# Gate products moved into the last recurrence, index transposes moved later, and gathers beside the dense group paced by the TensorE time of each piece

## The chip, the cores and the metric

The kernel runs on one core of one Trainium2 chip. The metric is device time in microseconds, of one execution of the whole program. The core has five engines with a queue of their own each: TensorE (PE, with PEld for its weight loads), VectorE (DVE), ScalarE (ACT), GpSimd (POOL) and SyncE (SP, which here only issues transfers). An instruction waits at the head of its queue, and what is behind it on that engine waits too.

## The reference

One layer on 1024 tokens of 1024 channels: a gated MLP over chunks of 128 tokens (gMLP), a state-space branch (SSD) over the same chunks, a gated merge with layer norm, and a PEER layer: each token picks, per head, the 16 best of 128 x 128 experts by two sets of keys, and uses those rows of two tables of 16384 x 1024.

```python
h = x @ w_in[i]
uv, z, xbc, dt_raw, gate_pre = jnp.split(h, [o1, o2, o3, o4], axis=-1)
gates = jax.nn.sigmoid((gate_pre + b_gate[i])).reshape(bsz, s, N_BRANCHES, d)
ya = gmlp_branch(uv, ...) @ gm_w_out[i]
yb = ssd_branch(z, xbc, dt_raw, ...) @ ssd_w_out[i]
merged = gates[..., 0, :] * ya + gates[..., 1, :] * yb
x1 = layer_norm(DEEPNORM_ALPHA * x + merged @ w_o[i], ln1_g[i], ln1_b[i])
ch = peer(x1, peer_w_q[i], peer_k1[i], peer_k2[i], peer_u[i], peer_v[i])
ple_gate = jax.nn.sigmoid(x1 @ ple_w_gate[i] + ple_b_gate[i])
ple = ple_gate * (p[i] @ ple_w_proj[i])
x = layer_norm(DEEPNORM_ALPHA * x1 + ch + ple, ln2_g[i], ln2_b[i])
```

In the SSD branch a state passes from chunk to chunk, `h = dec * h + st`, and each of 16 pairs of heads needs the state ahead of its chunk. In `peer`, for each token, `act = gelu(u_tab[e] . x) * gate` over its 128 experts, and the output is the sum of `act * v_tab[e]`.

## The kernel before

The 1024 tokens go in three groups: two blocks of 128 tokens, three blocks, three blocks (`GROUPS`). The first two groups are "gather" groups: their PEER rows are fetched one per token by indirect transfers from POOL's queue (L803), 128 x 1024 f32 (0.524 MB) at a time, 128 of `peer_u` and 128 of `peer_v` for each of five blocks, 1280 in all. They land in a ring of 12 slots (`RING`). VectorE multiplies a `peer_u` row with the token (L822); a `peer_v` row goes through TensorE (`product`, L864), four rows at a time. The last group is "dense": it multiplies with all of both tables.

Every large product is done in three fp32r matmuls (`mm3`, L150): a weight tile is loaded by SP, split into `whi` on ScalarE (L146) and `wlo` on VectorE (L147). `channel_major` gives 128 channels by all tokens of a group in a bank of the PSUM pool `mm` (four banks), 24 matmuls; `token_major` gives tokens by 256 channels. Small transposes and products use the pool `mt` (two banks). Tile pools and the order on each engine come from a scheduler that goes by the order of the code as a priority; `tc.high_priority(offset=n)` moves an instruction n places ahead.

`front(gi)` is the program of a group, a generator: the gMLP branch (four products `w_v`; then the `dt` chain of the SSD branch, L261 to L310; eight products `w_u`, each with a small product `pm` into `mix`; eight of `w_g` with `gm_w_out`), the SSD branch (`make_bc`, `make_x`, `core_g`, `core`, for 16 head pairs j), the merge (L509 to L525: gate product `w_g[8 + j]`, sigmoid, times `rrow`, product `ssd_w_out[j, 1]`), `w_o` and layer norm, `ple_w_proj`, transposes of `x1` (L581), 16 products `w_q` with the 16 best keys of each (L590 to L600), and `ple`. `core(j)` has two halves: the first transposes `xs`, makes the states, runs the recurrence into `pv` (L447, with the state of the group before loaded into `pv[:, 0]`, L440) and multiplies `dec` (L453); the second (L461, L464) makes `y`. `rrow` gathers the squares of `y`; `ss` (L503) sums it over partitions after the last pair.

While a group's `front` runs, two other streams are woven in. `beside` steps `select` of the group before (its choice of experts, VectorE work ending in transposes of the index, L739 to L786), three steps at a time. And the main loop at the end of `block_kernel` adds each yielded cost times `SIDE[phase]` to `owed` and steps the gathers (`experts`) while `owed` is above zero; a gather costs 1.47. `UNIT` = 5.35 is the cost of a product over 512 tokens, so 4.01 for three blocks. What is left of `experts` after the last group runs behind it.

`experts` first takes 64 rows of `peer_u` (`PP`), and then merges each half block of `peer_v` with the next 64 of `peer_u`. `transposed` of `actd` (L786, L829) turns a half block's activations for TensorE.

`dense` (group 2, phase 4) goes over 16 blocks of 8 pieces. `piece(i2)` makes `ewh`, `ewl` of 128 experts: for 48 pieces (`AHEAD`, six blocks) the scores were stored in `s_d` earlier and are only loaded; for the others `channel_major(peer_uT)` computes them. In a step, the products `po` of a block with `peer_vd` (18 matmuls of 512 columns each, eight per step) take turns with the pieces of the next block. The six loaded blocks are spread among the ten computed ones: the steps that make the pieces of blocks 5, 4, 3, 2, 1 and 0 are steps 0, 2, 5, 8, 10 and 13. Weight, `s` and `gte` loads are issued by SP.

```python
while side and owed > 0:
    step = next(side[0], None)
    if step is None:
        side.pop(0)
    else:
        owed -= step
```

Of the kernel before, what the change touches and what calls it, by code (L numbers as in the profile page):

```python
# [8 lines left out]
F32 = mybir.dt.float32  # L9
# [46 lines left out]
def take(g, n):  # L56
    for _ in range(n):
        yield next(g)
# [20 lines left out]
def block_kernel(ctx, tc, a, out):  # L79
# [135 lines left out]
    def front(gi):  # L215
# [24 lines left out]
        with tc.tile_pool(name="ga", bufs=1, side=side_) as ga, \  # L240
# [9 lines left out]
            for u in range(4):  # L250
                for cc, p in token_major(a["w_v"][u], xh, xl):
                    A.activation(v[:, cc, u * 256:u * 256 + 256], p, AF.Gelu_apprx_tanh)
                for c in range(NB):
                    V.bn_stats(st[:, c, u, :], v[:, c, u * 256:u * 256 + 256])
                beside()
                yield 2 * unit

            with tc.tile_pool(name="sd", bufs=1, side=side_) as sd:
# [13 lines left out]
                sh = [128, NB, NCOL]  # L272
                dt = xp.tile(sh, F32, name="dt")
                V.tensor_add(dt, pd, dtb[:, None, :].to_broadcast(sh))
                e = sd.tile(sh, F32, name="e")
                A.activation(e, dt, AF.Abs)
                A.activation(e, e, AF.Exp, scale=-1.0)
                r = sd.tile(sh, F32, name="r")
# [4 lines left out]
                q = sd.tile(sh, F32, name="q")  # L283
# [5 lines left out]
                V.tensor_mul(e, dt, nega[:, None, :].to_broadcast(sh))  # L289
                pc = pst.tile([128, 2, NB * NCOL], F32, name="mt", tag="mt")  # L290
# [3 lines left out]
                acs = xp.tile(sh, F32, name="acs")  # L294
                acsf = acs.rearrange("p c h -> p (c h)")
                A.copy(acsf, pc[:, 0, :])
                cdec = xp.tile(sh, F32, name="cdec")
                A.activation(cdec.rearrange("p c h -> p (c h)"), pc[:, 1, :], AF.Exp)
                dtd = xp.tile(sh, F32, name="dtd")
# [6 lines left out]
                act = sd.tile([NB * NCOL, 128], F32, name="q")  # L306
                A.copy(act, pt)
                arow = dram.tile([NCOL, NB, 128], F32, name=f"arow{gi}")
# [13 lines left out]
            gl = ga.tile([128, 8, T], F32R, name="gl")  # L322
            for g in range(8):
# [40 lines left out]
        with tc.tile_pool(name="sa", bufs=1, side=side_) as sa, tc.tile_pool(name="sb", bufs=2, side=side_) as sb:  # L364
# [18 lines left out]
            bT, cT, xs, zs, arows, btok, cbm = [{} for _ in range(7)]  # L383
# [31 lines left out]
            def core(j):  # L415
# [23 lines left out]
                if gi > 0:  # L439
                    DMA.dma_start(pv[:, 0], state_d[gi - 1, j])  # L440

                for c in range(NB if gi < NG - 1 else NB - 1):
# [3 lines left out]
                    for h in range(2):  # L446
                        V.scalar_tensor_tensor(pv[:, (c + 1) % NB, h], pv[:, c, h],  # L447
# [10 lines left out]
                for c in range(NB):  # L458
                    for h in range(2):
# [3 lines left out]
                        if c + gi > 0:  # L463
                            PE.matmul(o, lhsT=pv[:, c, h, :], rhs=ce[:, h, c * 128:c * 128 + 128],  # L464
                                      start=False, stop=True, tile_position=(0, h * 64))
# [23 lines left out]

            yield from make_bc(0)  # L490
            yield from make_x(0)
            for j in range(16):
                if j % 2 == 1 and j < 15:
                    yield from make_bc(j // 2 + 1)
                if j < 15:
                    yield from make_x(j + 1)
# [15 lines left out]
        with tc.tile_pool(name="mb", bufs=2, side=side_) as mb:  # L512
            for j in range(8):
# [4 lines left out]
                pg = channel_major(a["w_g"][8 + j], xh, xl)  # L518
# [42 lines left out]
        with tc.tile_pool(name="qa", bufs=1, side=side_) as qa, tc.tile_pool(name="qb", bufs=2, side=side_) as qb:  # L561

            for c in range(NB):
# [5 lines left out]
                if mode == "gather":  # L569
# [550 lines left out]
```

## Time and profile before

| | us |
|---|---|
| median of 3 runs (lowest, highest) | 3779.35 (3778.96, 3787.96) |
| the profiled execution | 3774.55 |
| its span, first to last instruction | 3772.9 |
| TensorE busy | 3437.7 (91%) |
| VectorE busy | 2936.8 (78%) |
| ScalarE busy | 1756.0 (47%) |
| POOL busy | 1606.3 (43%) |
| mean granted clock of TensorE | 0.955 of full speed |

The busy time of an engine is the time in which it executed something, not a measure of how well. The clock is granted at one of two levels (1.2 and 2.4 GHz); 0.955 means that it was at the lower for 9% of the time. Group 0 ends near 500 us, group 1 near 1350 us; the dense group's products run from 2657.7 to 3757.3 us. The gathers run from 567 to 3662 us. 1184 MB are moved, 314 GB/s on average.

### The profile page before, as it was taken

The page shows a single profiled execution, that of the slowest core. Times are in us where ns is not written, and L with a number is a line of the kernel's source. Part 1 is how long each engine was busy: PE and PEld are TensorE (multiplying, and loading weights), DVE is VectorE, ACT ScalarE, POOL GpSimd, SP SyncE. Part 2 cuts the span into 40 slices and gives each one's busy share as a digit, 9 for nine tenths or more (in the row PEclk, how much of TensorE's full clock was granted, in tenths as well). Part 3 has the DMA queues.
Part 4 walks back from the last instruction along what each step waited for, and adds up shares of the span by engine and source line. Part 5 has one row for each costly group of instructions (what it writes and reads, how often), then busy time and mean ns, then how long its engine had stood idle before and what let it go on. Part 6 is the DMA issues. An engine that isn't in the chain of part 4 may idle for free.

```text
span 3772.9 us, 59493 instructions
## 1 busy us (share of the span) xinstructions
PE 3437.7 (91%) x21390; PEld 2946.2 (78%) x21390; DVE 2936.8 (78%) x6823; ACT 1756.0 (47%) x2675; POOL 1606.3 (43%) x1310
## 2 busy tenths in 40 slices
PE   8898997999989988999988989998889989989988
PEld 8897996988877876888878888777667868667756
DVE  6677799898977989896688999997667766766535
ACT  6788543476843333466652334774222323322223
POOL 0000004756545354554354445443556565665540
PEclk9998998999999988999989999999999999999999
DMA  5453656989879886989888899999999999999992
GB/s 200 161 172 130 238 180 241 389 309 356 317 279 385 309 324 234 356 311 343 305 326 327 298 338 349 362 377 372 360 381 400 395 386 389 368 383 401 356 350 95
DMA packets 409159, 1183.88 MB, mean 314 GB/s; under 512 B 41120, under 2 KB 139424, under 8 KB 405792
## 3 DMA queue, kind: packets, MB, share of 16 engines
q0 software_dynamic: 187488, 682.71, 47.7%
q1 hardware_dynamic: 221376, 497.38, 36.9%
q8 instruction: 168, 2.75, 0.3%
q14 instruction: 127, 1.04, 0.1%
HBM read 1121.01 MB, written 58.92 MB: 313 GB/s over the span
## 4 chain that ended last, share of the span: by engine, by line
PE 33%; DVE 16%; DMA 13%; issue 4%; ACT 1%; POOL 1%; SPq 0%; DVEq 0%; ACTq 0%; POOLq 0%
PE mm L152 6%; PE mm L154 6%; PE mm L153 6%; PE pacc L864 4%; DVE row L822 3%; DVE wlo L147 3%; DMA ew<-s 3%; PE po L152 3%; DMA row<-in_peer_v_dram,idxT 3%; PE po L153 3%; PE po L154 3%; DMA raw<-in_peer_uT_dram 2%; PE mt L947 2%; DMA row<-in_peer_u_dram,idx 1%; DMA raw<-in_peer_vd_dram 1%
## 5 line engine op out<-in xcount | busy, mean ns | idle before, releaser
L146 ACT CAST whi<-raw 128x1024 fp32r<-128x1024 f32 (+1 forms) x676 | 701.1, 1041 | 1192.4 <-PE mm L153 612.0
L803 POOL DMA_INDIRECT row<-in_peer_u_dram,idx x640 | 811.5, 1268 | 874.9 <-PE pacc L864 254.3
L147 DVE TENSOR_TENSOR wlo<-raw,whi 128x1024 fp32r<-128x1024 f32 (+1 forms) x676 | 816.2, 1210 | 375.5 <-ACT whi L146 374.7
L154 PE MATMUL mm<-xh,wlo 128*128 128x384 f32 (+2 forms) x3160 | 1056.4, 335 | 46.7 <-DVE wlo L147 46.7
L152 PE MATMUL mm<-xh,whi 128*128 128x384 f32 (+2 forms) x3160 | 1066.3, 338 | 34.3 <-ACT whi L146 25.6
L803 POOL DMA_INDIRECT row<-in_peer_v_dram,idxT x640 | 780.9, 1220 | 712.0 <-PE pacc L864 232.5
L153 PE MATMUL mm<-xl,whi 128*128 128x384 f32 (+2 forms) x3160 | 1051.9, 333 | 0.6 <-DVE xl L136 0.6
L822 DVE SCALAR_TENSOR_TENSOR row<-row,x1b 128x1024 f32<-128x1024 f32 x640 | 774.6, 1217 | 64.8 <-DMA row<-in_peer_u_dram,idx 58.5
L152 PEld LDWEIGHTS mm<-xh,whi 128*128 128x128 f32 (+1 forms) x3160 | 611.2, 194 | 89.7 <-ACT whi L146 46.1
L154 PEld LDWEIGHTS mm<-xh,wlo 128*128 128x128 f32 (+1 forms) x3160 | 609.8, 193 | 66.4 <-DVE wlo L147 55.0
L153 PEld LDWEIGHTS mm<-xl,whi 128*128 128x128 f32 (+1 forms) x3160 | 610.5, 193 | 12.2 <-issue 6.1
L864 PE MATMUL pacc<-row,zw 128*32 128x512 f32 x2560 | 316.9, 614 | 37.0 <-DMA row<-in_peer_v_dram,idxT 36.8
L152 PE MATMUL po<-whi,ewh 128*128 128x512 f32 x768 | 316.0, 411 | 32.2 <-DVE eacc L1013 32.2
L153 PE MATMUL po<-wlo,ewh 128*128 128x512 f32 x768 | 311.0, 405 | 14.4 <-DVE wlo L147 14.3
L154 PE MATMUL po<-whi,ewl 128*128 128x512 f32 x768 | 309.9, 404 | 0.0
L152 PEld LDWEIGHTS po<-whi,ewh 128*128 128x128 f32 x768 | 148.3, 193 | 104.6 <-DVE eacc L1013 36.1
L864 PEld LDWEIGHTS pacc<-row,zw 128*32 128x32 f32 x2560 | 67.9, 111 | 180.6 <-issue 131.1
L135 ACT CAST ewh<-ew 128x384 fp32r<-128x384 f32 x128 | 65.6, 514 | 296.7 <-DVE ew L985 230.1
L818 POOL DMA_DIRECT2D x1b<-x x5 | 3.0, 601 | 446.4 <-DMA x<-x 446.4
L153 PEld LDWEIGHTS po<-wlo,ewh 128*128 128x128 f32 x768 | 148.5, 193 | 51.0 <-DVE wlo L147 16.8
L154 PEld LDWEIGHTS po<-whi,ewl 128*128 128x128 f32 x768 | 148.1, 193 | 40.9 <-issue 5.0
L153 PE MATMUL mm<-wlo,xh 128*128 128x256 f32 x512 | 147.8, 289 | 11.4 <-DVE wlo L147 11.4
(272 smaller groups left out, 5603.8 us busy)
## 6 DMA issues: line engine op xcount, KB each, us to landing
raw<-in_peer_uT_dram SPq DMA_DIRECT2D x128, 512.0 KB, 8.0
raw<-in_peer_vd_dram SPq DMA_DIRECT2D x128, 512.0 KB, 6.8
raw<-in_w_xbc_dram SPq DMA_DIRECT2D x96, 512.0 KB, 5.9
raw<-in_w_g_dram SPq DMA_DIRECT2D x48, 512.0 KB, 6.7
raw<-in_w_z_dram SPq DMA_DIRECT2D x48, 512.0 KB, 5.4
raw<-in_ssd_w_out_dram SPq DMA_DIRECT2D x48, 512.0 KB, 5.3
raw<-in_w_q_dram SPq DMA_DIRECT2D x48, 512.0 KB, 4.7
g<-gt SPq DMA_DIRECT2D x24, 1024.0 KB, 7.5
```

Of the source, the lines that this page charges most:

```text
L135: A.copy(hi, src)
L146: A.copy(hi, raw)
L147: V.tensor_sub(lo, raw, hi.bitcast(F32))
L152: PE.matmul(p, lhsT=lh, rhs=rh, start=start, stop=False, skip_group_check=skip)
L153: PE.matmul(p, lhsT=lh, rhs=rl, start=False, stop=False, skip_group_check=skip)
L154: PE.matmul(p, lhsT=ll, rhs=rh, start=False, stop=stop, skip_group_check=skip)
L803: g = POOL.indirect_dma_start(out=t, out_offset=None, in_=a[tab], in_offset=bass.IndirectOffsetOnAxis(ap=ix, axis=0))
L818: POOL.dma_start(x1, x1_d[gi, c])
L822: u = V.scalar_tensor_tensor(t, t, 1.0, x1, op0=OP.mult, op1=OP.mult, accum_out=act[:, k:k + 1])
L864: return PE.matmul(pacc[q * 32:q * 32 + 32, h * 512:h * 512 + 512], lhsT=zws[z][:, q, r % 4, :], rhs=ts[q][:, h * 512:h * 512 + 512], star ...
L947: PE.matmul(p[:, i, :], lhsT=o1, rhs=o2, start=True, stop=True)
```

## The change

1. *The `dt` chain* becomes a generator `steps()`, and is stepped once behind each of the products `w_v[1]` to `w_v[3]`, and a last time behind `w_u[0]`.
2. *`w_u`*: the product of `g + 1` stands ahead of the small products of `g` (`make_u`).
3. *The state* of the group before is loaded in `make_x` into a tile of its own, `p0`, and no longer into `pv[:, 0]` in `core`.
4. *The merge's* first three gate products stand between the halves of `core(15)` and around it (`pgs`). Each yields one unit, and the merge's iterations yield two units as before.
5. *`x1`'s stores* are issued by ScalarE's queue, behind `ple_w_proj`; SP issued them inside the layer norm. `kT` is loaded in pairs, at high priority.
6. *`select`* has three more empty steps (`BESIDE`) ahead of its transposes.
7. *`experts`* takes six more rows of `peer_u` at the start.
8. *`dense`* yields 0.3 for a piece that is only loaded, and 4.01 for a computed one as before (`took`).

```diff
 def take(g, n):
     for _ in range(n):
-        yield next(g)
+        c = next(g, None)
+        if c is None:
+            return
+        yield c
...
+            def steps():
...
+                yield
                 pd = pst.tile([128, NB, NCOL], F32, name="mt", tag="mt")
...
+                yield
                 pc = pst.tile([128, 2, NB * NCOL], F32, name="mt", tag="mt")
...
+                yield
                 pt = pst.tile([NB * NCOL, 128], F32, name="mt", tag="mt")
                 PE.transpose(pt, acsf, ident)
...
+            staged = steps()
+            for u in range(4):
+                for cc, p in token_major(a["w_v"][u], xh, xl):
+                    A.activation(v[:, cc, u * 256:u * 256 + 256], p, AF.Gelu_apprx_tanh)
+                for c in range(NB):
+                    V.bn_stats(st[:, c, u, :], v[:, c, u * 256:u * 256 + 256])
+                beside()
+                if u > 0:
+                    next(staged)
+                yield 2 * unit
...
+            def make_u(g):
+                p = channel_major(a["w_u"][g], xh, xl)
+                ugs.append(gb.tile([128, T], F32, name="ug", tag="t1", bufs=3))
+                A.activation(ugs[g], p, AF.Gelu_apprx_tanh)
+
+            make_u(0)
+            next(staged, None)
             for g in range(8):
-                p = channel_major(a["w_u"][g], xh, xl)
-                ug = gb.tile([128, T], F32, name="ug", tag="t1", bufs=3)
-                A.activation(ug, p, AF.Gelu_apprx_tanh)
+                if g < 7:
+                    make_u(g + 1)
+                ug = ugs[g]
...
+                if gi > 0:
+                    pvs[j] = sb.tile([128, 2, 64], F32, name="p0")
+                    DMA.dma_start(pvs[j], state_d[gi - 1, j])
                 xs[j] = conv(channel_major(a["w_xbc"][j], xh, xl), j, "xs")
...
-                if gi > 0:
-                    DMA.dma_start(pv[:, 0], state_d[gi - 1, j])
+                p0 = pvs.pop(j, None)
...
-                        V.scalar_tensor_tensor(pv[:, (c + 1) % NB, h], pv[:, c, h],
+                        V.scalar_tensor_tensor(pv[:, (c + 1) % NB, h], (pv[:, c] if c else p0)[:, h],
...
+            tail = core(15)
+            for n in range(3):
+                pgs.append(channel_major(a["w_g"][8 + n], xh, xl))
+                yield unit
+                c = next(tail, None)
+                if c is not None:
+                    yield c
             ss = psm.tile([128, T], F32, name="mm")
...
-                pg = channel_major(a["w_g"][8 + j], xh, xl)
+                pg = pgs[j] if j < len(pgs) else channel_major(a["w_g"][8 + j], xh, xl)
...
-                if mode == "gather":
-                    x1_d[gi, c] = dram.tile([128, 1024], F32, name=f"x1_{gi}_{c}")
-                    DMA.dma_start(x1_d[gi, c], x1[:, c])
...
+            if mode == "gather":
+                for c in range(NB):
+                    x1_d[gi, c] = dram.tile([128, 1024], F32, name=f"x1_{gi}_{c}")
+                    A.dma_start(x1_d[gi, c], x1[:, c])
...
-                kT = qb.tile([128, 128], F32, name="kT", bufs=3)
-                DMA.dma_start(kT, a["kT"][:, u, :])
+                if u % 2 == 0:
+                    k2 = qb.tile([128, 2, 128], F32, name="kT")
+                    with tc.high_priority(offset=AHEAD_W[0]):
+                        DMA.dma_start(k2, a["kT"][:, u:u + 2, :])
+                kT = k2[:, u % 2]
...
-                transposed(ixT[:, p], pt[:, p * 128:p * 128 + 128], ixf)
...
+            for _ in range(BESIDE):
+                yield 0.5
+            pt = ps["mt"].tile([128, 512], F32, name="mt", tag="mt")
+            for p in range(PARTS):
+                transposed(ixT[:, p], pt[:, p * 128:p * 128 + 128], ixf[p])
...
-        yield from take(first, PP)
+        yield from take(first, PP + 6)
...
+            def took(i2):
+                return UNIT * NB / 4 if i2 >= sum(AHEAD) else 0.3
+
             for i in range(I2B):
                 piece(order[0] * I2B + i)
-                yield UNIT * NB / 4
+                yield took(order[0] * I2B + i)
...
-                            piece(order[step + 1] * I2B + h * I2B // 2 + i // 2)
-                            yield UNIT * NB / 4
+                            n = order[step + 1] * I2B + h * I2B // 2 + i // 2
+                            piece(n)
+                            yield took(n)
```

## Rows read from the trace of the kernel before

**Rows 1.** The page, part 1: busy us and share of the span.

```profile
PE 3437.7 (91%) x21390; PEld 2946.2 (78%) x21390; DVE 2936.8 (78%) x6823; ACT 1756.0 (47%) x2675; POOL 1606.3 (43%) x1310
```

**Rows 2.** Stretches of the dense group: length, busy us by engine, clock, DMA.

```profile
core 0: us, PE busy (x) PEld busy (x) DVE busy (x) ACT busy (x) POOL busy (x), PEclk, DMA share, GB/s
2657.70:3757.30 1099.60, 1013.47 (x5157) 771.23 (x5156) 687.12 (x1063) 308.93 (x410) 584.05 (x490) 0.96 0.95 359
2657.70:3632.50 974.80, 902.21 (x4614) 681.00 (x4613) 634.19 (x996) 271.99 (x365) 573.18 (x478) 0.96 1.01 383
2793.40:2854.70 61.30, 44.87 (x193) 30.07 (x193) 37.42 (x62) 12.90 (x18) 31.59 (x28) 0.83 0.99 372
3440.00:3470.00 30.00, 30.00 (x163) 23.98 (x162) 23.17 (x37) 9.24 (x13) 20.85 (x19) 1.00 1.03 405
3632.50:3723.40 90.90, 77.36 (x404) 63.28 (x401) 38.24 (x48) 28.15 (x35) 10.87 (x12) 0.92 0.61 221
```

**Rows 3.** Waits of PE in the dense group: us in total, times, longest.

```profile
PE pacc L864 <- DMA row<-in_peer_v_dram,idxT: 35.8, 12, 8.4
PE po L152 <- DVE eacc L1013: 32.2, 7, 13.5
PE po L153 <- DVE wlo L147: 14.3, 5, 5.2
```

**Rows 4.** Instructions in the dense group: busy us, mean ns, idle before.

```profile
L803 POOL DMA_INDIRECT row<-in_peer_v_dram,idxT x272 | 321.8, 1183 | 240.0 <-PE pacc L864 97.8 <-DVE row L822 68.3 <-issue 57.2
L864 PE MATMUL pacc<-row,zw 128*32 128x512 f32 x1120 | 142.7, 629 | 35.9 <-DMA row<-in_peer_v_dram,idxT 35.8
```

**Rows 5.** DVE in time, last gather block's finish: start, us, operation.

```profile
3682.11 1.21 DVE L768 TENSOR_TENSOR x1b<-x1b,pacc 128x1024 f32<-128x1024 f32 x1
3692.50 1.22 DVE L774 TENSOR_TENSOR x1b<-x1b,row 128x1024 f32<-128x1024 f32 x1
```

**Rows 6.** Waits of PE, 345 to 368 us (group 0).

```profile
PE mt L461 <- DVE dec L453: 4.4, 2, 2.8
```

**Rows 7.** Waits of PE, 1050-1080 us, then 1915-1945.

```profile
PE mt L461 <- DVE dec L453: 10.7, 1, 10.7
PE mm L503 <- DVE rrow L473: 3.9, 1, 3.9
...
PE mt L461 <- DVE dec L453: 9.2, 2, 8.8
PE mm L503 <- DVE rrow L473: 4.2, 1, 4.2
```

**Rows 8.** DVE in order of time, 1045 to 1080 us.

```profile
1067.00 0.28 DVE L447 SCALAR_TENSOR_TENSOR pv<-pv,cdec,mt 128x64 f32<-128x64 f32 x1 [6.32 <-DMA pv<-state]
```

**Rows 9.** Stretches with lowered clock or full DVE, columns as above.

```profile
1070.00:1090.00 20.00, 15.70 (x83) 14.28 (x84) 15.61 (x31) 6.86 (x8) 7.36 (x5) 0.80 0.66 220
1934.00:1960.00 26.00, 20.74 (x109) 19.77 (x110) 24.93 (x40) 8.61 (x11) 19.57 (x16) 0.79 0.97 352
1485.00:1515.00 30.00, 22.26 (x120) 19.99 (x119) 29.75 (x120) 7.06 (x8) 12.22 (x10) 0.79 0.60 223
560.00:640.00 80.00, 57.56 (x311) 51.55 (x311) 76.84 (x237) 31.73 (x47) 32.48 (x26) 0.86 0.66 237
```

**Rows 10.** Waits of PE, 1395 to 1500 us (start of group 2).

```profile
PE mt L786 <- DVE ixf L739: 8.8, 2, 7.1
PE mm L786 <- DVE actd L829: 7.0, 1, 7.0
```

**Rows 11.** Near 1200 us: waits of SP, of PE; ACT in time.

```profile
SPq L571 <- DVE x L568: 6.8, 3, 3.2
...
PE mt L581 <- DVE xl L136: 7.7, 1, 7.7
...
1213.60 1.04 ACT L146 CAST whi<-raw 128x1024 fp32r<-128x1024 f32 x1 [5.87 <-DMA raw<-in_w_q_dram]
```

**Rows 12.** Waits of PE, 555 to 640 us (group 1, w_u stage).

```profile
PE mt L271 <- ACT dtw L268: 5.5, 1, 5.5
```

More of the change, by code (lines that the diff above doesn't have):

```diff
@@ L249, in front @@
             st = ga.tile([128, NB, 4, 6], F32, name="st")
[L250 to L258, printed above, removed]
+            sh = [128, NB, NCOL]
+            dt, acs, cdec, dtd = [xp.tile(sh, F32, name=n) for n in ("dt", "acs", "cdec", "dtd")]
+            arow = dram.tile([NCOL, NB, 128], F32, name=f"arow{gi}")
+            def steps():
                 raw = wp.tile([128, KD, NCOL], F32, name="raw", tag="raw", bufs=4)
@@ L271, in front @@
                     PE.transpose(pd[:, c, :], dtw[:, c * 128:c * 128 + 128], ident[:NCOL, :NCOL])
-                sh = [128, NB, NCOL]
-                dt = xp.tile(sh, F32, name="dt")
                 V.tensor_add(dt, pd, dtb[:, None, :].to_broadcast(sh))
-                e = sd.tile(sh, F32, name="e")
+                e, r, q = [ga.tile(sh, F32, name=n) for n in ("e", "r", "q")]
                 A.activation(e, dt, AF.Abs)
                 A.activation(e, e, AF.Exp, scale=-1.0)
-                r = sd.tile(sh, F32, name="r")
                 V.tensor_scalar_add(r, e, 2.0)
@@ L381, in conv @@
                 return xc
-            bT, cT, xs, zs, arows, btok, cbm = [{} for _ in range(7)]
+            bT, cT, xs, zs, arows, btok, cbm, pvs = [{} for _ in range(8)]
             def make_bc(g):
@@ L463, in core @@
                         if c + gi > 0:
[L464 removed]
+                            PE.matmul(o, lhsT=(pv[:, c] if c else p0)[:, h, :], rhs=ce[:, h, c * 128:c * 128 + 128],
                                       start=False, stop=True, tile_position=(0, h * 64))
@@ L487, in first_half @@
                     yield unit
+            pgs = []
             yield from make_bc(0)
             yield from make_x(0)
-            for j in range(16):
-                if j % 2 == 1 and j < 15:
+            for j in range(15):
+                if j % 2 == 1:
                     yield from make_bc(j // 2 + 1)
-                if j < 15:
-                    yield from make_x(j + 1)
+                yield from make_x(j + 1)
                 if j % 2 == 0:
@@ L730, in select @@
         prf = pr.rearrange("p h k -> p (h k)")
-        pt = ps["mt"].tile([128, 512], F32, name="mt", tag="mt")
         if mode == "gather":
@@ L735, in select @@
             ixT = idxT_t[gi, c].rearrange("p (n q r) -> p n q r", n=PARTS, q=4)
+            ixf = [tk.tile([128, PARTS, PP], F32, name=f"ixf{p}") for p in range(PARTS)]
             for p in range(PARTS):
                 part = slice(p * PP, p * PP + PP)
-                ixf = tk.tile([128, PARTS, PP], F32, name="ixf")
-                V.scalar_tensor_tensor(ixf, twice(sel[0][:, part]), 128.0, twice(sel[1][:, part]),
+                V.scalar_tensor_tensor(ixf[p], twice(sel[0][:, part]), 128.0, twice(sel[1][:, part]),
                                        op0=OP.mult, op1=OP.add)
-                V.tensor_copy(idx_t[gi, c][:, part], ixf[:, 0])
-                transposed(ixT[:, p], pt[:, p * 128:p * 128 + 128], ixf)
+                V.tensor_copy(idx_t[gi, c][:, part], ixf[p][:, 0])
             gate_t[gi, c] = peer.tile([128, PAIRS], F32, name=f"gate{gi}_{c}")
             A.copy(gate_t[gi, c], prf)
-        else:
+            for _ in range(BESIDE):
[3 more added lines that the diff above has]
+                transposed(ixT[:, p], pt[:, p * 128:p * 128 + 128], ixf[p])
+        else:
+            for _ in range(BESIDE):
+                yield 0.5
+            pt = ps["mt"].tile([128, 512], F32, name="mt", tag="mt")
             for n, q in enumerate((sel[0], sel[1], prf)):
```

8 lines of the change are left out of this document (2 added, 6 removed).

## The prediction

> **What bounds the kernel now.** I read the busy shares first: TensorE is busy for 91% of the span [rows 1], so time can come back only where it idles or runs at half its clock. Then I split the span into stretches, and asked in each what TensorE waited for, which transfers and which queue stood behind that wait, and what the granted clock was.
>
> Two kinds of loss appear. In the dense group, from the first to the last of its 2304 products `po` (1099.6 us), the DMA engines have a busy share of 0.95, and of 1.01 until the gathers run out; there 383 GB/s are moved, and 405 GB/s in a stretch in which TensorE doesn't idle at all [rows 2]. TensorE is busy 1013.5 us of it, so it idles 86 us, nearly all put down to three waits: for a gathered row, for the adds into `eacc` and for `wlo` [rows 3]. Its clock averages 0.96, which is another 4% of 1099.6, or 44 us. So 130 of 1099.6 us are lost, and 970 us would be the same work without a loss.
>
> Ahead of that, TensorE stops at the seams between stages: at the end of the recurrences [rows 6 to 8], where group 2's selects are transposed [rows 10], after the first layer norm [rows 11] and at the `dt` chain [rows 12]. VectorE is full in some of these: 76.8 of 80 us, and 29.75 of 30 [rows 9].
>
> **The pacing in the dense group (`took`).** A yield of the main generator, times `SIDE[4]` = 0.78, is credit for the gathers, 1.47 each. A step of `dense` (one block of eight pieces) yields eight products and eight pieces of 4.01: 16 x 4.01 x 0.78 / 1.47 = 34 gathers, whatever the next block's pieces are. For six blocks the pieces are only loaded from `s_d`, and TensorE works on the products alone. Such a step asks for 34 x 0.524 MB of rows, 8 x 0.524 MB of `peer_vd`, 1.6 MB of `s` and 1.6 MB of `gte`: 25.2 MB, which is 62 us at 405 GB/s. The step at 2793 us lasted 61.3 us with TensorE busy for 44.9 and its clock at 0.83 [rows 2]: a stretch bound by transfers. With 0.3 for a loaded piece, such a step lets go (8 x 4.01 + 8 x 0.3) x 0.78 / 1.47 = 18 gathers, 16.8 MB, 42 us at 405 GB/s: about what TensorE needs.
>
> What isn't let go there must run later. Before, steps 0 to 13 let go 14 x 34 and step 14 the last 11, 487 in all. After, nine computed steps of 34, six loaded ones of 18 and 17 in the last step make 434. Merge also has three more yields of one unit in each of groups 1 and 2 (3 x 4.01 x 0.78 / 1.47 = 6 gathers each), so 475 are needed and some 42 remain when the code of the dense group ends. They run behind it with nothing beside them.
>
> The sum for this part: the 53 gathers that leave the dense stretch are rows of `peer_v`. 1120 matmuls take 142.7 us for 272 rows [rows 4], an upper bound of 0.52 us a row as they overlap, at most 28 us; I take 0.45, or 24. The floor of the dense stretch is then 970 - 24 = 946 us, and its ceiling with all 130 us of losses kept is 1076. By transfers: 1099.6 us at 359 GB/s are 395 MB; less 53 x 0.524 MB that is 367 MB, which is 958 us at 383 GB/s and 906 at 405 [rows 2]. The two demands come out nearly equal, so I don't take the floor: a third of the losses stays, 946 + 43 = 989 us. The tail: of 42 gathers some 8 are under way in the ring when the products end (12 slots, 2 held by the dense group's own norm rows). The other 34 go at 1.58 us (19 POOL instructions in 30 us, beside weights [rows 2]): 54 us; a lower bound is 1.2 us by their busy time [rows 4], 41 us. Behind it one landing (9 us by the same row's waits for rows, longest 8.4 [rows 3]), and the finish of a block, from its first add at 3682.1 to its last ending at 3693.7 [rows 5], 11.6 us, with a store behind it, 14 us in all. Together 77 us, at least 64. Before, 15.6 us followed the last product (3757.3 to the span's end of 3772.9). So 989 + 77 against 1099.6 + 15.6: 49 us less. The ends: 946 + 64 is 105 less, 1076 + 77 is 38 more. I take **-45 us**.
>
> A rule speaks against this: the Trainium skill's "DMA: Bandwidth & Descriptors", section Specifications, gives about 358 GB/s as a core's share of HBM. By it 395 - 6 MB would take 1087 us plus a finish, and this part would be worth some 15 us. The trace doesn't agree: 405 GB/s were moved in 30 us on end.
>
> **Gate products in the last recurrence, and the state's earlier load.** At the end of the recurrences nothing else is in line for TensorE. It waits 10.7 + 3.9 us in group 1, 9.2 + 4.2 us in group 2 [rows 7], 4.4 us in group 0 [rows 6]: 32 us. Of group 1's, VectorE itself waits 6.3 us for `pv<-state`, which could be issued only when the last head's `pv` was free [rows 8]; the separate tile `p0` is loaded a step earlier. Behind the waits the clock is down: 0.80 for 20 us and 0.79 for 26 us [rows 9], 9.5 us. So 41 us are to be had. Three products of 24 matmuls (4 us each; this is also what a unit stands for) lie across the recurrence, enough to cover 10 us waits. What the edit adds: three products and `ss` hold all four `mm` banks, so the next product waits until ScalarE has taken one, with a table load; no row shows this wait, I bound it between 0 and the 4.2 us of today's wait for `rrow`, and take 3 us in each group, 9 in all. The 6 extra gathers of each merge are 3 MB, 8 us of transfers at 405 GB/s; the stretch in group 2 has a DMA share of 0.97 [rows 9], so I charge 7 us once. `p0`'s load is queued on SP ahead of weights and waits for the head two back; those weights are the ones issued early, so 0. 41 - 9 - 7 = **-25 us** (0 to -41).
>
> **Transposes later, six gathers more, `x1` by ScalarE, `dt` within `w_v`, `w_u` one ahead.** Group 2 waits 8.8 us for `ixf` and 7.0 for `actd` [rows 10], and its clock of 0.79 over 30 us costs 6 [rows 9]. Later transposes remove the first unless VectorE is late anyway: it is full there, so I count half with the clock, 7 us. Six gathers of lead put `act` some 12 gathers ahead of its transpose, which is more than 7 us: 6. SP stands 6.8 us on `x1`'s stores, so `w_q` is late, ScalarE waits 5.87 us for it with the splits of `xh` behind, and TensorE 7.7 [rows 11]. ScalarE's queue now holds those stores behind `proj`, when `x1` has long been normalised; behind them stand the splits, and three issues cost about 1 us: 6 us. `dt`: 5.5 us [rows 12], where VectorE is full; 2. `w_u` one ahead, `kT` in pairs and the empty yields of `select` remove no wait of size here: 0, and -2 to 2. I keep 21, and of it 18, since a stall removed ahead of a full VectorE partly returns: **-18 us** (0 to -30).
>
> The Trainium skill would say less of the stores: in "DMA: Bandwidth & Descriptors", section Issuing engines are not separate DMA queues, DMAs from several engines share the same 16 DMA engines, and issuing elsewhere saves only issue time. By it the move gains about 1 us. The rows show an issue held up by a wait, not bandwidth, so I keep 6.
>
> **The sum.** The profiled execution took 3774.55 us, its span 3772.9; the median of the runs is 4.8 us above. -45 - 25 - 18 = -88 us: 3686 on the profiled execution, 3691 on the median.
>
> **Rivals.** *The tail eats the dense group's gain.* If the dense stretch falls only to 1038 us (70% of its losses stay, since VectorE and ScalarE wait in order for `ew` and `raw`), 77 us of tail make it level. For: two of the three waits name VectorE, not a row [rows 3]. Against: that VectorE waited behind transfers. Then 3779 - 43 = 3736.
>
> *The seams keep their time.* VectorE is full at several [rows 9], and four full banks replace the wait for `rrow`. Then the dense group alone: 3779 - 45 = 3734.
>
> *Slower: the bare tail.* The 42 gathers cost 77 us against today's 15.6 at a point where nothing runs beside them. If fewer gathers don't cure the loaded steps at all, the dense stretch stays at 1076, this part is +38, and with a third of the seams (-14) the time is 3803. It decides from a dense stretch above 1038 + 14 + 11 = 1063 us. Against: 34 gathers in such a step are more than 405 GB/s can carry.
>
> *It doesn't do what it says.* Transfers have a share of 0.97 at group 2's merge already [rows 9] and are full in the dense group, so whatever is removed returns as a wait for rows, and the gathers held back are paid in full at the end: 3775 or a little above.
>
> **How the numbers follow.** Forecast 0.55 (3650 to 3730 by itself), tail level 0.17, seams kept 0.13, slower 0.08, nothing 0.07. The predicted time is 3691. The range takes in the forecast and both half-gains with a little on each side, 3640 to 3760, and leaves out the last two. 0.3% (11 us) is about what can be told from no change: faster 0.85, same 0.07, slower 0.08.
>
> **What would show it.** Loaded steps near 42 us instead of 61, few waits of `pacc` for rows in them; gathers right up to the end, and some 75 us from the last `po` to the end of the span; no wait of VectorE for `state`; the waits for `dec` and `rrow` under 3 us. Wrong if the tail passes 90 us, if loaded steps still idle 10 us, or if a wait for an `mm` bank of 5 us or more stands in each merge.

## The result, and the profile after

The changed kernel takes 3759.23 us (median of 6 runs, 3748.88 to 3764.2) against 3786.53 us of the kernel before (6 runs, three of which are those of the table above the prediction): a ratio of 0.9927, 95% interval 0.9911 to 0.9943, some 27 us faster. The forecast was 88 us faster. The time lies in the stated range by less than 1 us, the direction is right, and the gain is less than a third of what was forecast.

The chips differ: the kernel before took 3784 to 3788 us in three of the comparisons of this document and 3760 to 3763 us in three others, on other chips. So each experiment below is given as a ratio to the kernel before on the same chip. For this first comparison, and for the traces of [rows 1 to 12] and of the changed kernel here, the chip isn't on record; where traces of different chips are set against each other below, it is said.

Stretches of the changed kernel (columns as in [rows 2]): the dense products, one step with loaded pieces, and what follows the last product.

```profile
core 0: us, PE busy (x) PEld busy (x) DVE busy (x) ACT busy (x) POOL busy (x), PEclk, DMA share, GB/s
2664.10:3673.00 1008.90, 971.67 (x4953) 762.30 (x4955) 671.75 (x1036) 305.95 (x406) 520.32 (x439) 0.98 0.97 364
2779.30:2832.40 53.10, 41.55 (x181) 29.90 (x178) 32.42 (x55) 11.47 (x16) 22.32 (x20) 0.87 0.99 361
3673.00:3752.60 79.60, 34.76 (x193) 6.47 (x192) 15.25 (x29) 5.63 (x7) 38.83 (x40) 0.68 0.77 291
```

The dense products take 1008.9 us where they took 1099.6 [rows 2], and 79.6 us follow the last of them where 15.6 did. Of TensorE's waits in the dense products the one for gathered rows is gone, and the other two are halved or as they were [rows 3]; behind the products the wait for rows is back:

```profile
PE po L155 <- DVE eacc L1051: 17.9, 4, 8.6
PE po L156 <- DVE wlo L150: 17.0, 4, 8.8
...
PE pacc L898 <- DMA row<-in_peer_v_dram,idxT: 33.3, 10, 7.0
```

At the seams, TensorE's waits in the changed kernel, in this order: end of group 1's recurrences (1030 to 1070 us), of group 2's (1890 to 1925), start of group 2 (1380 to 1500), start of group 1 (545 to 640).

```profile
PE mm L527 <- DVE rrow L489: 0.7, 1, 0.7
...
PE mm L157 <- DVE wlo L150: 5.0, 2, 4.0
...
PE mm L157 <- DVE wlo L150: 9.4, 6, 3.9
PE mm L155 <- ACT whi L149: 3.2, 3, 1.6
PE mt L290 <- DVE e L286: 2.8, 1, 2.8
...
PE mm L157 <- DVE wlo L150: 14.2, 1, 14.2
PE mt L343 <- ACT v L195: 7.5, 1, 7.5
```

The waits that the change was to remove are gone from these traces, which may be of two chips: 14.6 us in group 1's last recurrence are 0.7, 13.4 us in group 2's are replaced by 5.0 for `wlo`, and `ixf` and `actd` [rows 7, 10] don't lead the list any more. But `wlo`, VectorE's share of every weight, stands there now, and where group 1 waited 5.5 us for `dtw` [rows 12] it waits 14.2 for `wlo` and 7.5 for the normalised `v`.

The first product of the dense group begins at 2664.1 us, later than in the trace of before (2657.7), although the last `dec` product of group 2 had come 20 us earlier (1916.7 against 1937.0). The gates stage between them took 255.8 us in this trace and 234.1 in that one. On one chip (the pair below) it takes 254.6 us in the changed kernel and 251.4 in the kernel before, so in that pair the change accounts for 3 us; most of the difference is between chips (last section).

### The profile page after: what moved, and what is told of

The parts are those of the page before. It is cut to its first block, busy times and chain, and to the rows that moved or that the text cites. A ratio compares the mean times of both kernels' runs of the same rounds, so it can differ in the third digit from the quotient of the medians.

```text
span 3752.6 us, 59429 instructions
## 1 busy us (share of the span) xinstructions
PE 3439.9 (92%) x21390; PEld 2939.4 (78%) x21390; DVE 2935.7 (78%) x6823; ACT 1754.2 (47%) x2671; POOL 1569.2 (42%) x1310
## 5 line engine op out<-in xcount | busy, mean ns | idle before, releaser
L837 POOL DMA_INDIRECT row<-in_peer_u_dram,idx x640 | 796.3, 1244 | 1004.3 <-PE pacc L898 376.2
L837 POOL DMA_INDIRECT row<-in_peer_v_dram,idxT x640 | 758.9, 1186 | 681.9 <-DVE row L856 210.9
L155 PEld LDWEIGHTS mm<-xh,whi 128*128 128x128 f32 (+1 forms) x3160 | 606.9, 192 | 93.4 <-ACT whi L149 51.5
L981 PE MATMUL mt<-o,o 128*128 128x128 f32 x768 | 148.9, 302 | 15.1 <-DVE o L979 6.0
```

The source lines that it names most:

```text
L155: PE.matmul(p, lhsT=lh, rhs=rh, start=start, stop=False, skip_group_check=skip)
L837: g = POOL.indirect_dma_start(out=t, out_offset=None, in_=a[tab], in_offset=bass.IndirectOffsetOnAxis(ap=ix, axis=0))
L981: PE.matmul(p[:, i, :], lhsT=o1, rhs=o2, start=True, stop=True)
```

## The experiments

Each kernel ran in three or more rounds beside the kernel before on the same chip.

**Both kernels once more, on one chip.** No edit.

> The kernel before once more, for a trace of it on this chip. The ratio is 1. My theory of the pacing, that it alone gains nothing, rests on a dense stretch of the kernel before that is shorter on this chip than the 1099.6 us of the first trace; some 1088 us are expected. Rival: 1100 us again; then the pacing alone must have lost elsewhere.

> The changed kernel once more, beside the others on one chip, for a second trace of it. My theory: the 16 us that its first trace lost in the stage of the gates (2335 to 2470 us) belong to that execution, and here the dense group starts some 25 us earlier than in the kernel before, as in the version with all but the pacing; 0.993 of the kernel before. Rival: the loss in the gates comes back, as a part of the change.

Measured: 0.9999 (0.9983 to 1.0015), and 0.9935 (0.9913 to 0.9956). The dense products of the kernel before, those of the changed kernel, and what follows them:

```profile
2676.80:3769.90 1093.10, 1018.78 (x5157) 775.93 (x5156) 687.47 (x1063) 309.13 (x410) 587.90 (x490) 0.96 0.95 362
...
2669.30:3680.90 1011.60, 973.02 (x4954) 762.38 (x4956) 671.36 (x1036) 306.27 (x406) 520.97 (x439) 0.98 0.97 363
3680.90:3761.20 80.30, 32.99 (x192) 6.34 (x192) 15.25 (x29) 5.63 (x7) 38.97 (x40) 0.72 0.77 289
```

So on one chip the change is 7.5 us ahead when the dense products begin (2669.3 against 2676.8), these take 81.5 us less, and 64.8 us more follow them (80.3 against 15.5): 24 us in all, as the times of these two executions say (3762.92 and 3787.13). My expectation of a lead of 25 us fell: in this pair it is 18 us at the last `dec` product of group 2 (1924.1 against 1942.3), 9 at its last `kT` product (2170.4 against 2179.4), and the stages behind that change it by 4 us at most. On the chip of the next experiments the lead is there: the dense products begin at 2657.2 us in the program of before (the kernel with the pacing alone), at 2635.5 and 2631.2 in the new one (all but the pacing, and the same with other pacing). These last two are the same program up to there and 4 us apart, so one trace doesn't tell a lead to better than some us.

**The pacing alone, and all but the pacing.** The first is the kernel before with `took`, the second the changed kernel with

```diff
-                return UNIT * NB / 4 if i2 >= sum(AHEAD) else 0.3
+                return UNIT * NB / 4
```

> The kernel before with the pacing of the loaded pieces alone (0.3 for a piece that is only loaded). My theory: the pacing carries what the change gained. The dense stretch shortens by about as much as in the changed kernel (1099.6 to some 1005 us), and 54 instead of 42 gathers stand behind it, so that some 98 us follow the last product instead of 79.6. In all about -14 us against the kernel before (-5 to -25). Rival: the pacing only breaks even and the seams pay; then 0 to +10 us here.

> The changed kernel with 4.01 for every piece, so everything but the pacing. My theory: the waits at the seams go and the lead of up to 28 us is lost again before the dense group, where VectorE is full; the dense group is as before. In all -5 to +5 us against the kernel before. Rival: the seams pay what they removed (some 27 us), and what was lost before the dense group in the changed kernel's profile was chance; then -20 to -30 us here.

Measured: 0.9996 (0.9979 to 1.0012) for the pacing alone, 0.9950 (0.9933 to 0.9966) for all the rest. My theory falls in both and the rival holds, in the second at its low end (19 us where it said 20 to 30): the pacing by itself gains nothing, and the seams pay. The pacing alone, dense products and what follows:

```profile
2657.20:3665.10 1007.90, 968.41 (x4922) 761.89 (x4924) 680.06 (x1047) 305.62 (x406) 515.19 (x438) 0.98 0.98 365
3665.10:3760.10 95.00, 41.80 (x241) 8.00 (x240) 15.75 (x33) 5.62 (x7) 50.09 (x52) 0.75 0.81 310
```

The dense products are as short as in the changed kernel, and 95 us of bare gathers pay it all back.

**The same gathers, all within the dense group.** The changed kernel with

```diff
-SIDE = (0.82, 0.78, 0.80, 0.66, 0.78)
+SIDE = (0.82, 0.78, 0.80, 0.66, 0.856)
```

> The changed kernel with SIDE of the dense group at 0.856 instead of 0.78, so that by count all gathers are let go before the code of the dense group ends. My theory: beside the products a gather costs TensorE 0.5 us, behind them 1.5 us and a landing; the dense stretch grows by 20 to 30 us and what follows the last product falls from 79.6 to 20 or 30 us: 25 to 35 us below the changed kernel, some -55 us against the kernel before. Rival: the transfers are full in the dense stretch, so that 42 gathers more cost there what they cost behind it; then the same as the changed kernel, -27 us.

Measured: 3700.51 us, 0.9839 (0.9798 to 0.9879). The theory holds in the gain. Dense products and rest, first of all but the pacing, then of this one, from one chip:

```profile
2635.50:3729.80 1094.30, 1007.09 (x5141) 770.16 (x5140) 680.43 (x1048) 309.19 (x410) 561.91 (x479) 0.96 0.94 355
3729.80:3745.70 15.90, 0.00 (x1) 0.00 (x0) 9.27 (x17) 4.09 (x5) 0.00 (x0) 0.66 0.25 99
...
2631.20:3681.70 1050.50, 1001.25 (x5129) 769.30 (x5132) 674.13 (x1039) 305.19 (x406) 561.94 (x478) 0.97 0.98 369
3681.70:3700.80 19.10, 1.86 (x17) 0.35 (x16) 13.84 (x25) 5.52 (x7) 0.00 (x0) 0.69 0.27 110
```

These two kernels have the same program up to the dense group and let all gathers go within it; one lets go 34 in each step by count, the other 20 or 37. That alone makes the dense products 43.8 us shorter. So the mechanism of the pacing was right, and it is worth what was forecast, if nothing is left behind. Against the pacing alone (434 by count, on the same chip) the 476 gathers let go here lengthen the dense products by 42.6 us, 1.0 us each, twice the 0.5 that I had expected; behind the products the 50 that the trace of the pacing alone has there cost 95.0 - 19.1 = 76 us, 1.5 us each.

**The extra credit of merge.** The changed kernel with

```diff
                 split(mh[:, j], ml[:, j], ya)
-                yield 2 * unit
+                yield (1 if j < len(pgs) else 2) * unit
```

then the merge part (gate products, `p0`) alone with and without the credit on the kernel before, and the whole without the pacing and without the credit.

> The changed kernel, the first three merge iterations yielding one unit instead of two, so that merge lets go as many gathers as before (6 fewer in each of groups 1 and 2). My theory: in group 2's merge VectorE is full, and 6 rows of peer_u at 1.2 us lengthen it by 7 us; that stretch becomes some 7 us shorter than in the changed kernel, and the 12 gathers more behind the dense group cost 18 us: in all 5 to 15 us slower than the changed kernel. Rival: merge is longer since three products and ss hold the four banks; then that stretch keeps its length and the kernel is 18 us slower than the changed one.

> The kernel before with the merge's first three gate products in the last recurrence and the state's earlier load, and nothing else; its extra yields let 6 more gathers go in each of groups 1 and 2. My theory: the waits at the three ends go (some 7, 15 and 15 us), and in group 2's merge 6 rows of peer_u on a full VectorE give back some 13 of them: -15 us against the kernel before (-5 to -22), with the lead lost in the stretch from the last recurrence of group 2 to the first w_q product. Rival: nothing of it lasts (0), as the other seams take it up.

> The same without the extra credit: the first three merge iterations yield one unit, so that as many gathers go as before. My theory: the lead of some 30 us is kept through group 2's merge, and the dense group is as before: -25 us against the kernel before, and 8 to 15 us below the version with the credit. Rival, that merge grew because three products and ss hold the four banks: the lead is lost there all the same, and the two versions are alike.

> The changed kernel without the pacing and with merge's first three iterations yielding one unit. My theory: the credit costs here what it cost with merge alone, 0.4%: 0.991 of the kernel before, some -33 us. Rival: with the other parts in, the credit's price is gone; 0.995 as with it.

Measured: in the changed kernel 0.9928 (0.9908 to 0.9949) without the credit, 31 us below the kernel before, though 54 instead of 42 gathers stand behind the products: level with the changed kernel (0.9927 and 0.9935 on other chips), not 5 to 15 us above it. By these ratios, what the credit costs ahead of the dense group it saves behind the products. The merge part alone: 0.9998 (0.9984 to 1.0012) with the credit, as the rival had it, 0.9959 (0.9942 to 0.9976) without. The whole without pacing and credit: 0.9929 (0.9904 to 0.9954), between my theory and its rival. From VectorE's last multiplication of `dec` in group 2 to ScalarE's first copy of a `w_q` product, the merge part with and then without the credit, on one chip:

```profile
1909.10:2074.80 165.70, 135.12 (x832) 123.21 (x832) 150.72 (x251) 50.02 (x71) 84.78 (x67) 0.92 0.93 339
...
1900.60:2058.30 157.70, 125.00 (x763) 116.89 (x762) 142.00 (x232) 50.22 (x71) 82.52 (x60) 0.91 0.90 325
```

VectorE is busy for 91% and 90% of it; with the credit it has 8.7 us more to do and the stretch is 8.0 us longer. At its start the version with the credit is 8.5 us behind. Group 1's merge has the same yields, but this lag isn't made there: behind it, the last product with `kT` of group 1 comes at 1285.3 us with the credit and at 1284.1 without. Nor does the lag of 16.5 us at the end of the stretch last: where the gates begin 2 us of it are left (2324.2 against 2322.2), where the dense products begin 11 (2642.8 against 2631.8). So the credit takes 15 us by the times, the whole gain of the merge part: gathers were let go by a yield whose product had been moved away. Where it takes them is only in part shown. That the four `mm` banks hold merge up, the rival, isn't seen. Without the credit the lead lasts, and in the changed kernel the longest wait for a bank that ScalarE frees at the three ends is this, in group 2, behind `ss`:

```profile
PE mm L155 <- ACT rrow L528: 2.2, 1, 2.2
```

**The other parts alone**, on the kernel before: the `dt` chain within `w_v` and `w_u` one ahead; the stores of `x1` on ScalarE's queue; `select`'s later transposes with six gathers of lead; `kT` in pairs.

In `dt`'s part the chain is cut into pieces by `yield` and drawn on between `w_v`'s products; the edits are these, in the order named (`-` is the kernel before):

```diff
+            sh = [128, NB, NCOL]
+            dt, acs, cdec, dtd = [xp.tile(sh, F32, name=n) for n in ("dt", "acs", "cdec", "dtd")]
...
+                if u > 0:
+                    next(staged)
                 yield 2 * unit
```

```diff
-                if mode == "gather":
-                    x1_d[gi, c] = dram.tile([128, 1024], F32, name=f"x1_{gi}_{c}")
-                    DMA.dma_start(x1_d[gi, c], x1[:, c])
...
+            if mode == "gather":
+                for c in range(NB):
+                    x1_d[gi, c] = dram.tile([128, 1024], F32, name=f"x1_{gi}_{c}")
+                    A.dma_start(x1_d[gi, c], x1[:, c])
```

```diff
-                transposed(ixT[:, p], pt[:, p * 128:p * 128 + 128], ixf)
...
+            for _ in range(BESIDE):
+                yield 0.5
+            pt = ps["mt"].tile([128, 512], F32, name="mt", tag="mt")
+            for p in range(PARTS):
+                transposed(ixT[:, p], pt[:, p * 128:p * 128 + 128], ixf[p])
...
-        yield from take(first, PP)
+        yield from take(first, PP + 6)
```

```diff
-                kT = qb.tile([128, 128], F32, name="kT", bufs=3)
-                DMA.dma_start(kT, a["kT"][:, u, :])
+                if u % 2 == 0:
+                    k2 = qb.tile([128, 2, 128], F32, name="kT")
+                    with tc.high_priority(offset=AHEAD_W[0]):
+                        DMA.dma_start(k2, a["kT"][:, u:u + 2, :])
+                kT = k2[:, u % 2]
```

> The kernel before with the dt chain within w_v and w_u one product ahead, alone. My theory: the waits for dtw (5.5 us) and mix (3.6 us) go, and part of it returns on a full VectorE: -5 us against the kernel before (0 to -10). Rival: what is removed is given back at the next seam: 0.

> The kernel before with the stores of x1 on ScalarE's queue behind ple_w_proj, alone. My theory: the wait of 7.7 us near 1208 goes and stays gone: -6 us against the kernel before (-2 to -12). Rival: the stores only change their queue and ScalarE's splits wait instead: 0 or slower by 1 us.

> The kernel before with the later transposes of select and the six gathers of lead alone. My theory: the waits for ixf (8.8 us) and actd (7 us and 3 us) go, half of it lasts where VectorE is full: -8 us against the kernel before (-3 to -15). Rival: VectorE is the limit where these waits stood, so 0.

> The kernel before with kT loaded in pairs at high priority, alone. If this edit holds what the other parts don't explain, 0.995 of the kernel before (-15 to -20 us), by fewer and earlier issues on SP. My theory: it removes no wait of TensorE and SP waits longer for its two buffers; 0 (-4 to +4), and the missing gain is in the parts acting together.

Measured: 0.9977 (0.9964 to 0.9991), 1.0005 (0.9991 to 1.0018), 1.0016 (1.0004 to 1.0027) and 1.0000 (0.9985 to 1.0014). Only the first gains, some 9 us by the ratio (3 to 14 by its interval). TensorE's waits where the third was to remove some (1380 to 1500 us, [rows 10]), and where the second was (1190 to 1235 us, [rows 11]):

```profile
PE mm L157 <- DVE wlo L150: 11.4, 7, 3.5
PE mm L155 <- ACT whi L149: 5.5, 7, 1.0
...
PE pacc L865 <- DMA row<-in_peer_v_dram,idxT: 3.0, 1, 3.0
PE mm L153 <- DVE wlo L147: 1.8, 1, 1.8
```

The waits named are gone in both, and the time of the kernel is as before or longer. The two stretches, first at the start of group 2 in the program of before (pacing alone) and with the later transposes, from two chips with the same time of the kernel before; then near the `x1` stores in the kernel before and with the stores moved, from one chip:

```profile
1380.00:1500.00 120.00, 89.06 (x526) 72.64 (x519) 114.53 (x381) 43.08 (x64) 55.39 (x40) 0.89 0.69 249
...
1380.00:1500.00 120.00, 100.43 (x607) 83.30 (x600) 116.09 (x367) 46.82 (x68) 59.28 (x47) 0.94 0.78 279
...
1190.00:1235.00 45.00, 37.79 (x254) 30.57 (x254) 37.85 (x77) 17.12 (x29) 27.54 (x26) 0.92 1.02 399
1190.00:1235.00 45.00, 37.48 (x266) 29.02 (x254) 36.46 (x61) 15.41 (x27) 27.22 (x24) 0.92 1.01 392
```

With the later transposes TensorE does get through more work there (100.4 against 89.1 us busy), though VectorE is at 95% and 97%. With the stores moved it doesn't: VectorE is at 81%, but the transfers have a share of 1.01, and TensorE now waits for rows and others.

**Where the leads go.** The lead of each version can be read where the dense products begin. All but the first line have the dense group of before, with 470 to 481 gathers in it by trace; all come from chips on which the kernel before takes 3760 to 3763 us, one trace each.

| version | first dense product at, us | dense products take, us | time against the kernel before, us |
|---|---|---|---|
| pacing alone (old program up to there) | 2657.2 | | -3 |
| pairs of `kT` alone | 2660.5 | 1088.5 | +2 |
| later transposes and lead alone | 2647.5 | 1100.7 | +6 |
| merge part, with the credit | 2642.8 | 1097.0 | -1 |
| merge part, without the credit | 2631.8 | 1096.2 | -16 |
| all but the pacing | 2635.5 | 1094.3 | -19 |
| all but pacing and credit | 2622.1 | 1099.9 | -23 |
| all but pacing, `kT` one by one | 2633.3 | 1087.1 | -24 |

So the seams do win time up to the dense group: the later transposes 10 to 13 us, the merge part 14 to 18 with the credit and 25 to 29 without it, all together 35 to 38 without it. In all but the last line the dense products then take 6 to 12 us longer than in the version with `kT` alone, and part of the lead is gone at the end. Whether the lead lengthens them isn't shown: the kernel before itself took 1093.1 and 1099.6 us there on other chips, and these are single traces.

**The pairs of `kT`, taken out.** The whole without the pacing and with `kT` one by one, and the same without the credit too:

> The changed kernel without the pacing and with kT loaded one by one. If the pairs hold the missing gain: 1.000 of the kernel before. My theory: as with all parts but the pacing, 0.995.

> The changed kernel without the pacing, without merge's extra credit and with kT loaded one by one: only the parts that should remove waits at the seams. My theory: the seams are worth what was forecast for them, some 40 us, and the credit and the pairs took half of it: 0.990 of the kernel before. Rival: the pairs cost nothing and the difference was chance between chips: 0.993.

Measured: 0.9924 (0.9900 to 0.9948), below the 0.995 that I had expected, on a chip where the kernel before takes 3760 us, and 0.9962 (0.9945 to 0.9979), where it takes 3788. The second should have been the lower one. So the chip decides more here than the pairs, and whether these cost anything is open; alone they do nothing.

**Gathers let go earlier, and versions faster than both.** Without the credit, with `SIDE[4]` at 0.876; without it, with `SIDE` = (0.82, 0.84, 0.80, 0.66, 0.83); and the latter with `kT` one by one (the credit and `kT` as in the diffs above):

```diff
-SIDE = (0.82, 0.78, 0.80, 0.66, 0.78)
+SIDE = (0.82, 0.78, 0.80, 0.66, 0.876)
```

```diff
-SIDE = (0.82, 0.78, 0.80, 0.66, 0.78)
+SIDE = (0.82, 0.84, 0.80, 0.66, 0.83)
```

> The changed kernel without the extra credit in merge and with SIDE of the dense group at 0.876, so that by count all gathers are let go before its code ends. My theory: both losses are independent, so the lead of 48 us at the start of the dense group and a dense group with nothing behind it add up: about 10 us below the version with 0.856 alone, -70 us against the kernel before. Rival: the 12 gathers moved into the dense group cost there what they cost in merge; then the same as with 0.856 alone, -62 us.

> The changed kernel without merge's extra credit, SIDE of the SSD and merge stages 0.84 instead of 0.78 and of the dense group 0.83, so that by count the last gather is let go with the last product of the dense group. My theory: gathers are cheaper in the SSD recurrences of group 2, where VectorE is at 0.75, than in the dense group: 10 us below the version with 0.876, 0.983 of the kernel before. Rival: merge, which has the same SIDE and a full VectorE, loses what the dense group wins: 0.985.

> The version with the gathers spread (no extra credit, SIDE 0.84 in the SSD and merge stages and 0.83 in the dense group), with kT loaded one by one. By the theory that the pairs cost 0.25%: 0.980 of the kernel before. Rival, that they cost nothing: 0.983.

Measured: 3706.63 us, 0.9853 (0.9825 to 0.9881); 3697.07 us, 0.9829 (0.9805 to 0.9853); 3744.02 us, 0.9875 (0.9854 to 0.9896), the last where the kernel before takes 3788 us. The first is no better than 0.856 alone, and its interval leaves out the 70 us of my theory, so the two cures don't add up. Its dense products take 1066.2 us (2618.8 to 3685.0) against 1050.5, by traces of two chips: the 12 gathers taken out of merge seem to cost in the dense group what they cost in merge. The second is the fastest measured, 63 us below the kernel before; its interval overlaps that of 0.856 alone, and the third says nothing of it, being on another chip.

## Why the prediction was right in direction and wrong in size

**The pacing: the mechanism right, two terms mis-sized.** The loaded steps were bound by transfers, and fewer gathers in them shorten the dense products by 81.5 us on one chip (forecast: 989 against 1099.6, 111). The tail of 77 us was right (80.3), and by its terms: 38 gathers go out behind the last product, 1.6 us each, and 21 us follow the last of them. The step that failed is "a third of the losses stays, 946 + 43 = 989 us": 1011.6 us were measured, TensorE idles 39 of them, and a clock of 0.98 is another 20. I had let the rate hold at 383 GB/s or more; it is 363, and a loaded step still takes 53 us with a DMA share of 0.99, not 42. With 11.5 us of it idle on TensorE, this is one of the prediction's own signs of being wrong.

Behind it lies a count that I took from the credit and not from the row: a loaded step was to ask for 34 gathers before and 18 after. The row of before has 28 of POOL's instructions and 372 GB/s in 61.3 us [rows 2], 22.8 MB and not 25.2; the row of after has 20 and 361 GB/s, 19.2 MB and not 16.8. What a loaded step couldn't move ran in the step behind it (48 gathers in one of them, where the credit of a step is 34), so that the change takes work out of the computed steps too: in the pair of one chip a loaded step fell from 58.6 to 51.5 us on the mean, a computed one from 78.2 to 72.8 (each from the last add into `eacc` of the step before it to its own). Added to that, this chip's dense products took 6.5 us less before. A forecast of -49 (cut to -45) became -17 in the changed kernel, and nothing for the pacing alone with 54 gathers left; the 12 gathers between them, at 1.5 us, are about the difference, and merge's credit had let them go for its 15 us. My rival "the tail eats the dense group's gain" named it and had a chance of 0.17. I priced a gather in the dense group at its 0.45 us of TensorE; the experiments give 1.0 us there. That the rest is the transfers that TensorE's weights wait for is likely where these are full, but not shown.

**The merge: the mechanism right, the price of one edit too low.** In the changed kernel the waits for `dec`, `state` and `rrow` go, and 16 us last with the merge part alone and no credit (forecast: 32 us of waits and 9.5 of clock, less 16). I charged the extra yields 7 us, as transfers; they cost 15, which eats the gain of the part. That they cost it as rows of `peer_u` on a full VectorE fits the one stretch read; [rows 9] showed VectorE at 24.9 of 26 us there. The wait for an `mm` bank, charged 9 us, is 2.2 us at the largest.

**The other seams: the step from a wait removed to time gained failed.** Forecast -18 us for the lot. `dt` and `w_u`, put at 2 us, gain 9. The `x1` stores, put at 6, gain nothing: transfers are full there. The later transposes with the lead, put at 13, are 10 to 13 us ahead where the dense products begin, and lose 6 in all. Of the stores, the sentence from the Trainium skill's "DMA: Bandwidth & Descriptors", section Issuing engines are not separate DMA queues, by which the stores on another queue would gain 1 us, came nearer (0.9991 to 1.0018 of the kernel before) than my 6 us. The trace agrees with it in so far as the transfers have a share of 1.01 there and TensorE is busy no longer than before, though SP's wait did go (7.5 us on that chip).

**What the sum missed.** Each seam was read at the wait that TensorE ended with, and what it won was carried to the end of the kernel unchanged. I didn't ask what else is full in the stretch (at the stores, the transfers), nor whether a lead made ahead of the dense group still counts behind it; in most of these versions it lasts only in part (table above).

**What stays open.** The parts alone sum to about 0 (0.9998, 0.9977, 1.0005, 1.0016, 1.0000), all but the pacing together gives 0.9950, on different chips. Whether the parts help each other or the chips account for it wasn't settled, nor what lengthens the dense products behind a lead, nor what the pairs of `kT` cost. Ratios may not carry over from chip to chip either: the spread version is at 0.9829 on one chip and, with `kT` one by one, at 0.9875 on another. The changed kernel itself wasn't run on a chip on which the kernel before takes 3760 us.

## What to carry to other kernels

When work that paces a side stream is moved, move its yield too, and count what is left of the stream at the end: pacing a stream down pays only as far as the rest still fits beside the main work, and rows left over cost 1.5 us each where they cost 1.0 beside it. Before a wait is priced as a gain, look at what else is full in that stretch, the transfers too. And a lead read at one seam has to be followed to the end: on one chip 18 us at 1924 us were 7.5 us at 2669, and by the traces of others a lead of 10 us at the first dense product had become a loss of 6 us at the end.

## What the runs showed of the hardware that I had not expected

The chips of the experiments differ by 0.7% on the kernel before, and much of it is in one place. The gates stage, from the first copy of `gt` to the last, in the kernel with the pacing alone (the same program as the kernel before up to the dense group) and in the kernel before on another chip:

```profile
2348.60:2584.10 235.50, 219.17 (x1417) 183.57 (x1417) 230.26 (x775) 178.71 (x322) 100.04 (x91) 0.99 0.95 362
...
2353.90:2605.30 251.40, 227.31 (x1418) 188.19 (x1419) 232.04 (x777) 179.33 (x324) 101.04 (x91) 0.97 0.91 344
```

The same instructions take 15.9 us longer, with 344 instead of 362 GB/s and a clock of 0.97 instead of 0.99, while VectorE and ScalarE are busy for as long as on the other chip within 2 us. In the twelve traces from the three chips on which the kernel before takes 3760 to 3763 us this stretch is 234 to 240 us, in the six from the two chips on which it takes 3784 to 3788 it is 246 to 258, whichever kernel ran. It doesn't account for every difference: the trace of [rows 2] has 234.1 us in this stretch, and its kernel took 3779 us in the runs beside it; there the dense products are the longer part (1099.6 us against 1088.5 with `kT` alone). What in the chip does it wasn't looked into.
